# Queries, gates and output projection multiplied as three passes over split operands, with two weight areas lent to the split parts

## The chip, the cores and the metric

The kernel runs on one core of one Trainium2 chip. The time is the device time of one execution in microseconds (us), as the median of three runs. The profile is of one further execution, taken by the hardware profiler. Engines are called by their names in the profile: PE is the matrix engine (PEld are its weight loads), DVE the vector engine, ACT the scalar engine, POOL the general engine, SP the engine that issues the weight transfers.

## The reference, cut to what matters

One transformer block on 256 tokens of 1024 features, all in float32. Queries, two gates and the output projection are plain matrix products; a mixture of 32 experts follows, of which each token uses 4, and every expert's weights (12 MB) are read.

```python
p = h @ w_in[l]                                   # keys and values, then queries and gates
q_a, q_b, g_a, g_b = split_qg(p[..., KV_COLS:])   # 512, 512, 1024, 1024 columns
...
y_a = global_attn(q_a, ...);  y_b = window_attn(q_b, ...)
x = x + g1 * (sigmoid(g_a) * (y_a @ w_br_a) + sigmoid(g_b) * (y_b @ w_br_b)) @ w_o
h2 = modulate(rms_norm(x, norm2_g[l]), sh2, sc2)
x = x + g2 * moe(h2, ...)                         # for e in range(32): t @ w_e1[e] ... act @ w_e2[e]
return rms_norm(x, final_g)
```

## The kernel before

**The stream of weights.** All weights go through a ring of areas in on-chip memory, each 128 x 4096 floats (2 MB), filled in a fixed order (`pieces`) by the SP queue. `N_PAIR = 8` areas are there from the start, each split in two halves of 1 MB; a front piece (`m0`, `q`, `in`, `mod`, `br`, `wo`) takes one half, an expert piece (`w1`, `w2`) a whole area. `done()` gives a piece's place back and `pump()` issues the next transfer into it, in program order; SP then waits until the last reader of that place has finished. After the attention `grow(xx)` and `grow(ptt)` add two more areas, so the experts run on ten.

**The front, in program order.** (1) The modulation `m0_prod(j)`/`m0_turn(j)` makes the scaled input `x[:, j, :]`, two rows of the loop ahead, between the query products `q_prods(j)`: 8 rows j x 8 column groups, each a product of a 128x128 weight block with 128x256 of x. (2) `q_chunk` rotates the queries on DVE while PE makes `gate(0)` and `gate(1)`; then keys (`proj`) and values. (3) `gate(2)` to `gate(8)`; a gate is 8 products of 128x128 by 128x256 and a Tanh on ACT. (4) The attention loop over u = 0 to 7 and two query halves qt: `turn` transposes the probabilities, `scores(u + 1, qt)` makes the next ones (maximum on DVE, Exp on ACT), `y_steps` finishes the last head pair, `weigh(u - 1)`, half a gate, `norm_p` (a reciprocal on DVE that needs the Exp's sums), and the share of the second modulation matrix (`mod_v` on DVE, `mod_p` on POOL and `mod_a` on ACT). (5) `br_prod`/`merge` multiplies the heads by `w_br`, weighs with the gates and leaves M. (6) The output projection: 8 groups m of 8 products, with `stats(m)` one group behind. (7) Routing, `gather`, and the experts: `gemm1`, `act`, `gemm2`, `scatter`.

Every engine runs its instructions in program order (`manual_schedule`); waits are semaphores that the framework sets from the data. A float32 product shows as two MATMUL records in the trace, each with its own weight load.

## Time and profile before

| what | value |
|---|---|
| median of 3 runs | 1195.11 us (1194.88 to 1195.83) |
| the profiled execution, its own time | 1195.13 us |
| its span, first to last instruction | 1193.4 us |
| PE busy | 1142.9 us (96%) |
| DVE, ACT, POOL busy | 359.4, 139.5, 35.7 us |
| moved by DMA | 458.34 MB, mean 384 GB/s |

The busy time of PE counts overlapping records once and their ends are modelled, so a busy PE is not yet a PE that sets the end. Between the span and the execution's own time lie 1.7 us, which are kept as they are.

### The profile page before, as it was taken

Reading aid. Unit: us, or ns where it says so; the run is one execution under the profiler, and the core shown is the slowest. Engines: PE = TensorE matmul, PEld = TensorE weight load, DVE = VectorE, ACT = ScalarE, POOL = GpSimd, SP = SyncE. Lnnn points to the kernel's source line nnn. Section 1 sums busy time; section 2 is a strip of 40 time slices with the busy share of each in tenths; the row PEclk is TensorE's granted clock in tenths of the full one; section 3 lists DMA queues with packets and bytes.
Section 4 is the critical chain, followed back from the end, with each engine's and each line's share of the span. In section 5 each row is a group of like instructions: output and inputs, shape, how many; then the busy total and the mean of one; then the engine's idle time right before and its main releaser. Section 6 shows DMA issues by size and latency. Waiting matters only on the chain.

```text
span 1193.4 us, 13447 instructions
## 1 busy us (share of the span) xinstructions
PE 1142.9 (96%) x5722; PEld 539.0 (45%) x5722; DVE 359.4 (30%) x767; ACT 139.5 (12%) x313; POOL 35.7 (3%) x31
## 2 busy tenths in 40 slices
PE   7999999999999999999999999999898989899996
PEld 5888666884434333443434343434232424233334
DVE  3274666332122232222232222222221212121222
ACT  2122554012000000000000000000000000000012
POOL 0232000000000000000000000000000000000001
PEclk9999999999999999999999999999999999999999
DMA  9995634948999999999999999999999999999994
GB/s 378 383 387 211 225 128 153 390 177 351 427 429 426 428 426 428 429 427 428 426 429 426 429 426 428 427 428 428 428 427 427 428 428 426 429 427 429 425 428 181
DMA packets 37952, 458.34 MB, mean 384 GB/s; under 512 B 4600, under 2 KB 4992, under 8 KB 7424
## 3 DMA queue, kind: packets, MB, share of 16 engines
q1 hardware_dynamic: 36144, 454.05, 91.0%
q10 hardware_dynamic: 1744, 3.38, 0.7%
q8 instruction: 47, 0.77, 0.3%
q14 instruction: 17, 0.14, 0.0%
HBM read 456.36 MB, written 1.05 MB: 383 GB/s over the span
## 4 chain that ended last, share of the span: by engine, by line
PE 57%; DMA 36%; DVE 4%; ACT 2%; issue 1%; ACTq 0%; SPq 0%; DVEq 0%
DMA ring<-w 26%; PE u L845 20%; DMA xx<-w 10%; PE y L884 9%; PE mm L375 3%; PE xg L812 3%; PE u L695 3%; PE qa L276 2%; PE o L705 2%; PE sp L901 2%; PE br L579 2%; ACT xx L517 1%; PE yl L985 1%; PE kp L365 1%; PE vp L449 1%; DVE st L507 1%
## 5 line engine op out<-in xcount | busy, mean ns | idle before, releaser
L845 PE MATMUL u<-ring,t 128*64 128x512 f32 x1632 | 373.8, 598 | 16.1 <-DMA ring<-w 15.7
L845 PEld LDWEIGHTS u<-ring,t 128*64 128x64 f32 x1632 | 112.6, 137 | 233.3 <-issue 201.2
L884 PE MATMUL y<-ring,r_q 128*64 128x512 f32 x768 | 168.9, 592 | 0.0
L891 DVE TENSOR_TENSOR t<-y,r_kv 64x512 f32<-64x512 f32 x60 | 41.3, 689 | 325.3 <-PE y L884 324.9
L884 PEld LDWEIGHTS y<-ring,r_q 128*64 128x64 f32 x768 | 55.2, 137 | 109.6 <-issue 107.9
L858 DVE TENSOR_SCALAR r_q<-u 128x512 f32<-128x512 f32 x32 | 22.1, 692 | 248.6 <-PE u L845 248.6
L860 ACT ACTIVATE r_q<-r_q 128x512 f32<-128x512 f32 x32 | 20.1, 629 | 510.0 <-DVE r_q L858 510.0
L695 PE MATMUL u<-mtx,keep 128*64 128x512 f32 x256 | 62.2, 604 | 3.0 <-DVE r_q L861 3.0
L812 PEld LDWEIGHTS xg<-mtx,r_y 128*128 128x128 f32 x512 | 58.4, 192 | 12.2 <-issue 12.2
L812 PE MATMUL xg<-mtx,r_y 128*128 128x128 f32 x512 | 61.3, 278 | 0.0
L375 PE MATMUL mm<-xx,ring 128*128 128x256 f32 x256 | 59.9, 385 | 0.0
L901 PE MATMUL sp<-t,mtx 128*128 128x512 f32 x120 | 59.7, 620 | 0.0
L375 PEld LDWEIGHTS mm<-xx,ring 128*128 128x128 f32 x256 | 47.3, 190 | 12.6 <-issue 5.0
L845 PE MATMUL u<-xx,t 128*64 128x512 f32 x208 | 48.7, 610 | 3.7 <-DMA xx<-w 3.6
L845 PE MATMUL u<-ptt,t 128*64 128x512 f32 x208 | 48.8, 598 | 0.9 <-DMA ptt<-w 0.9
L814 DVE TENSOR_TENSOR t<-xg,modb 128x512 f32<-128x512 f32 x32 | 22.1, 692 | 86.3 <-PE xg L812 86.3
L901 PEld LDWEIGHTS sp<-t,mtx 128*128 128x128 f32 x120 | 20.5, 191 | 39.5 <-issue 39.5
L902 DVE TENSOR_TENSOR r_t<-r_t,sp 128x512 f32<-128x512 f32 x60 | 38.3, 680 | 0.0
L695 PEld LDWEIGHTS u<-mtx,keep 128*64 128x64 f32 x256 | 16.3, 135 | 44.6 <-issue 22.6
L874 ACT COPY r_q<-ta 128x512 f32<-128x512 f32 x32 | 18.8, 586 | 146.6 <-PE ta L871 146.6
L276 PE MATMUL qa<-xx,ring 128*128 128x256 f32 x128 | 30.7, 388 | 0.0
L845 PEld LDWEIGHTS u<-xx,t 128*64 128x64 f32 x208 | 14.7, 139 | 35.3 <-issue 28.1
(229 smaller groups left out, 897.4 us busy)
## 6 DMA issues: line engine op xcount, KB each, us to landing
ring<-w SPq DMA_DIRECT2D x149, 2048.0 KB, 32.4
xx<-w SPq DMA_DIRECT2D x19, 2048.0 KB, 31.0
ptt<-w SPq DMA_DIRECT2D x19, 2048.0 KB, 32.4
ring<-w_mod SPq DMA_DIRECT2D x16, 1024.0 KB, 11.2
ring<-w_in SPq DMA_DIRECT2D x10, 1024.0 KB, 9.1
ring<-w_m SPq DMA_DIRECT2D x8, 1024.0 KB, 12.6
ring<-w2l SPq DMA_DIRECT2D x3, 2048.0 KB, 34.3
ring<-w_q SPq DMA_DIRECT2D x8, 512.0 KB, 12.1
```

What stands on the lines that cost most here:

```text
L276: nc.tensor.matmul(qa[c // 4][:, c % 4, :], w[:, 128 * c:128 * c + 128], x[:, j, :], start=(j == 0 and c % 2 == 0), stop=(j == 7), skip_gr ...
L375: nc.tensor.matmul(gp[0][:, 0:256], w[:, k, :], x[:, k, :], start=(k == 0), stop=(k == 7))
L579: nc.tensor.matmul(ps[:, 0:256], w[:, k, 128 * (m % 2):128 * (m % 2) + 128], Y[:, 4 * br + k, :], start=(k == 0), stop=(k == 3))
L695: nc.tensor.matmul(u[c0:c0 + 64, ch % 2, :], ident[:, 4 * e + ch:4 * e + ch + 1].to_broadcast([128, 64]), be1, start=True, stop=False)
L705: nc.tensor.matmul(ps[:, 0:256], w[:, k, :], M[:, k, :], start=(k == 0), stop=(k == 7))
L812: nc.tensor.matmul(xp[:, b, :], z[:, tb, 128 * k:128 * k + 128], S[:, tb, :], start=(tb == 0), stop=(tb == 1))
L814: nc.vector.tensor_tensor(out=XT[p][:, 4 * h:4 * h + 4, :], in0=xp, in1=sh2[:, 4 * h:4 * h + 4].unsqueeze(2).to_broadcast([128, 4, 128]), ...
L845: nc.tensor.matmul(u[c0:c0 + 64, ch % 2, :], XT[p][:, k, 64 * j:64 * j + 64], w[:, 512 * ch:512 * ch + 512], start=False, stop=(k == 7))
L884: nc.tensor.matmul(y[64 * h:64 * h + 64, :], l, w[:, 512 * h:512 * h + 512], start=(k == 0), stop=(k == 7))
L891: nc.vector.tensor_tensor(out=YY[p][64 * j:64 * j + 64, 512 * h:512 * h + 512], in0=y[64 * h:64 * h + 64, :], in1=g2[64 * h:64 * h + 64, 5 ...
L901: nc.tensor.matmul(sp, t[:, tb, :], y[:, s], start=True, stop=True)
L902: nc.vector.tensor_tensor(out=ACC[0][:, tb, s], in0=ACC[0][:, tb, s], in1=sp, op=ALU.add)
```

## The change

Each operand x, the 32 weight pieces concerned, and M are split into an upper part, a copy by ACT into the type `float32r`, and a lower part, the remainder, which DVE subtracts. `mm3` makes each product as three matmuls in that type: upper by upper, upper by lower, lower by upper. The parts of weights lie in two buffers of 128 x 2048 in turn (`upper`, `prep`), made one group before they are used; a weight piece is given back to the ring as soon as its last part is made. Keys, values, `w_br` and the experts stay float32. The parts take 32 KB of a partition, which are two of the ring's areas: `N_PAIR` falls to 6 and the two come back as `more0` and `more1` after the output projection. In the attention loop `mod_v` now stands before `norm_p`.

```diff
-N_PAIR = 8
+N_PAIR = 6
...
+    room = ExitStack()
     fr = ExitStack()
+    fz = fr.enter_context(tc.tile_pool(name="fz", bufs=1))
...
+    cut = {}
+    X3 = [fz.tile([128, 2048], F32R, name=n, tag=f"part{i}").rearrange("p (k c) -> p k c", k=8)
+          for i, n in enumerate(("x_hi", "x_lo"))]
...
+    def lower(lo, v, hi):
+        nc.vector.tensor_tensor(out=lo, in0=v, in1=hi.bitcast(F32), op=ALU.subtract)
...
+    def upper(kind, idx, b, pool):
+        w = take(kind, idx)[:, 1024 * b:1024 * b + 1024]
+        hl = parts(None, 2, "part", 2 + n_cut[0] % 2, pool)
+        n_cut[0] += 1
+        nc.scalar.copy(out=hl[:, 0, :], in_=w)
+        cut[kind, idx, b] = hl
+
+    def prep(kind, idx, b):
+
+        w, hl = take(kind, idx)[:, 1024 * b:1024 * b + 1024], cut[kind, idx, b]
+        lower(hl[:, 1, :], w, hl[:, 0, :])
+        if b or kind == "q":
+            done(kind, idx)
...
+    def mm3(ps, lt, rt, start, stop, **kw):
+        nc.tensor.matmul(ps, lt[0], rt[0], start=start, stop=False, **kw)
+        nc.tensor.matmul(ps, lt[0], rt[1], start=False, stop=False, **kw)
+        nc.tensor.matmul(ps, lt[1], rt[0], start=False, stop=stop, **kw)
...
+        nc.scalar.copy(out=X3[0][:, j, :], in_=x[:, j, :])
+        lower(X3[1][:, j, :], x[:, j, :], X3[0][:, j, :])
...
     crow_half(0)
     crow_half(1)
+    upper("q", 0, 0, fz)
+    prep("q", 0, 0)
     for k in range(8):
...
     for j in range(8):
         if j < 6:
             m0_prod(j + 2)
+        if j < 7:
+            upper("q", j + 1, 0, fz)
         q_prods(j, range(4))
+        if j < 7:
+            prep("q", j + 1, 0)
         if j < 6:
             m0_turn(j + 2)
         q_prods(j, range(4, 8))
-        done("q", j)
...
+    gate_up(0)
+    gate_low(0)
     q_chunk(0)
+    gate_up(1)
     q_chunk(1)
+    gate_low(1)
     gate(0)
...
     gate(3)
+    gate_up(5)
+    gate_low(5)
     mod_a()
     gate(4)
...
     scores(0, 0)
     gate(7)
     scores(0, 1)
+    gate_low(8)
+    gate_up(9)
     mod_v()
     norm_p(0, 0)
     norm_p(0, 1)
+    gate_low(9)
     gate(8)
...
             nc.vector.tensor_tensor(out=M[:, m, :], in0=M[:, m, :], in1=dst, op=ALU.add)
+            nc.scalar.copy(out=M3[0][:, m, :], in_=M[:, m, :])
+            lower(M3[1][:, m, :], M[:, m, :], M3[0][:, m, :])
...
+            if u < 7 and qt:
+                gate_low(10 + u)
+            mod_v()
             if u < 7:
                 norm_p(u + 1, qt)
-            mod_v()
+            if not qt:
+                gate_up(10 + u)
...
     for m in range(2, 8):
+        if m in (2, 5):
+            upper("wo", 0, m // 4, mz)
         merge(1, m)
+        if m in (2, 5):
+            prep("wo", 0, m // 4)
...
         pend = (m, zt)
+        if m < 6:
+            upper("wo", m // 2 + 1, m % 2, mz)
+            prep("wo", m // 2 + 1, m % 2)
...
+    room.close()
+    lz = late.enter_context(tc.tile_pool(name="lz", bufs=1, reuse_waits="tile"))
+    for i in range(2):
+        grow(lz.tile([128, 4096], F32, name=f"more{i}"))
```

## Rows read from the trace of the kernel before

**Rows 1.** The page: 40 slices of the span for PE, DMA and bandwidth.
```profile
PE   7999999999999999999999999999898989899996
...
DMA  9995634948999999999999999999999999999994
GB/s 378 383 387 211 225 128 153 390 177 351 427 429 426 428 426 428 429 427 428 426 429 426 429 426 428 427 428 428 428 427 427 428 428 426 429 427 429 425 428 181
```

**Rows 2.** Windows by stage: stretch, length, busy of PE, PEld, DVE, ACT, POOL; clock, DMA.
```profile
19.10:55.50 36.40, 36.40 (x236) 28.78 (x233) 9.76 (x31) 4.91 (x12) 6.15 (x4) 1.00 0.96 387
...
97.50:124.00 26.50, 26.50 (x120) 21.49 (x120) 8.28 (x14) 9.60 (x21) 7.06 (x3) 1.00 0.77 278
124.00:196.30 72.30, 69.66 (x442) 47.18 (x441) 47.21 (x99) 38.06 (x99) 2.37 (x1) 1.00 0.45 161
...
232.70:264.70 32.00, 32.00 (x173) 28.70 (x172) 10.81 (x29) 4.48 (x13) 0.00 (x0) 1.00 0.51 196
...
730.00:1138.00 408.00, 387.53 (x1802) 141.97 (x1798) 95.32 (x178) 19.62 (x35) 0.00 (x0) 1.00 1.01 427
```

**Rows 3.** Windows around the first expert product, same columns.
```profile
265.00:275.00 10.00, 9.99 (x80) 7.64 (x81) 5.00 (x27) 6.54 (x14) 0.22 (x1) 1.00 0.90 340
275.00:277.60 2.60, 2.60 (x16) 0.89 (x14) 2.36 (x13) 0.00 (x0) 0.00 (x0) 1.00 0.02 9
277.60:279.60 2.00, 2.00 (x12) 0.61 (x10) 0.00 (x0) 0.00 (x0) 0.00 (x0) 1.00 0.71 131
```

**Rows 4.** The chain that ended last, in order of time: start, length, what.
```profile
97.49 17.27 PE mm L375 x80
...
222.35 10.36 PE br L579 x48
...
248.60 3.46 PE o L705 x16
...
270.50 3.57 PE xg L812 x32
274.08 7.02 PE u L845 x32
```

**Rows 5.** The same chain, later.
```profile
823.24 39.08 DMA ring<-w
```

**Rows 6.** Groups of instructions by shape, first 290 us: busy us, mean ns, idle before.
```profile
L375 PEld LDWEIGHTS mm<-xx,ring 128*128 128x128 f32 x256 | 47.3, 190 | 12.6 <-issue 5.0 <-ACT t L377 0.8 <-ACT xx L517 0.8
...
L333 DVE SCALAR_TENSOR_TENSOR ring<-ring,crow 128x1024 f32<-128x1024 f32 x22 | 26.3, 1211 | 0.0
...
L346 ACT ACTIVATE ring<-ring 128x1024 f32<-128x1024 f32 x10 | 10.6, 1063 | 0.0
...
L377 ACT ACTIVATE t<-mm 128x256 f32<-128x256 f32 x16 | 6.2, 390 | 17.9 <-PE mm L375 17.9
...
L238 ACT COPY msb<-mp 128x256 f32<-128x256 f32 x8 | 3.0, 373 | 28.6 <-PE mp L235 24.8 <-issue 3.7
...
L587 DVE TENSOR_TENSOR r_t<-r_t,t 128x256 f32<-128x256 f32 x8 | 3.4, 425 | 0.3
```

**Rows 7.** Timeline of the start: start, length, engine, line, instruction.
```profile
15.75 0.42 DVE L266 TENSOR_TENSOR xx<-xx,rinv 128x256 f32<-128x256 f32 x1
...
17.01 0.59 ACT L257 COPY crow<-cps 128x512 f32<-128x512 f32 x1 [1.25 <-PE cps L255]
...
19.11 1.99 PE L276 MATMUL qa<-xx,ring 128*128 128x256 f32 x8
```

**Rows 8.** Timeline of two half turns in the attention loop, u = 3 to 4.
```profile
165.70 0.37 ACT L558 COPY r<-y 128x256 f32<-128x256 f32 x1
...
166.10 0.42 DVE L559 TENSOR_TENSOR r_y<-y,r 128x256 f32<-128x256 f32 x1 [1.75 <-ACT r L558]
...
166.71 1.21 DVE L333 SCALAR_TENSOR_TENSOR ring<-ring,crow 128x1024 f32<-128x1024 f32 x1
...
169.97 0.69 ACT L517 ACTIVATE xx<-s,st 128x512 f32<-128x512 f32 x1 [2.10 <-DVE st L512]
...
171.54 0.16 DVE L526 TENSOR_TENSOR st<-st 128x2 f32<-128x2 f32 x1 [1.49 <-ACT st L520]
...
171.82 1.20 DVE L333 SCALAR_TENSOR_TENSOR ring<-ring,crow 128x1024 f32<-128x1024 f32 x1
```

More of the change, by code (lines that the diff above doesn't have):

```diff
@@ L273, in q_prods @@
     def q_prods(j, cs):
-        w = take("q", j)
+        w = cut["q", j, 0]
         for c in cs:
-            nc.tensor.matmul(qa[c // 4][:, c % 4, :], w[:, 128 * c:128 * c + 128], x[:, j, :],
-                             start=(j == 0 and c % 2 == 0), stop=(j == 7), skip_group_check=True)
+            mm3(qa[c // 4][:, c % 4, :], [w[:, i, 128 * c:128 * c + 128] for i in range(2)], [v[:, j, :] for v in X3],
+                start=(j == 0 and c % 2 == 0), stop=(j == 7), skip_group_check=True)
     hc_pend = []
@@ L372, in gate_half, with gate_up, gate_low @@
             gp[0] = ps1.tile([128, 512], F32, name="mm", tag=tag, bufs=bufs)
-        w = take("in", i)[:, 1024 * b:1024 * b + 1024].rearrange("p (k c) -> p k c", k=8)
+        w = parts_of("in", i, b)
         for k in range(4 * n, 4 * n + 4):
-            nc.tensor.matmul(gp[0][:, 0:256], w[:, k, :], x[:, k, :], start=(k == 0), stop=(k == 7))
+            mm3(gp[0][:, 0:256], [v[:, k, :] for v in w], [v[:, k, :] for v in X3], start=(k == 0), stop=(k == 7))
         if n:
             nc.scalar.activation(out=tanh[m // 4][:, m % 4, :], in_=gp[0][:, 0:256], func=AF.Tanh, scale=0.5)
-            if b:
-                done("in", i)
+    def gate_up(m):
+        if m < 16:
+            upper("in", 2 + m // 2, m % 2, fz)
+    def gate_low(m):
+        if m < 16:
+            prep("in", 2 + m // 2, m % 2)
     def gate(m):
@@ L469, in tile_dit_block @@
     values(2)
+    gate_up(2)
+    gate_low(2)
     mod_p()
@@ L472, in tile_dit_block @@
     values(3)
+    gate_up(3)
+    gate_low(3)
     mod_v()
@@ L476, in tile_dit_block @@
     gate(2)
+    gate_up(4)
+    gate_low(4)
     mod_v()
@@ L479, in tile_dit_block @@
     gate(3)
+    gate_up(5)
+    gate_low(5)
     mod_a()
     gate(4)
+    gate_up(6)
+    gate_low(6)
     mod_v()
     gate(5)
+    gate_up(7)
+    gate_low(7)
     mod_v()
@@ L486, in tile_dit_block @@
     gate(6)
+    gate_up(8)
     mod_p()
```

15 lines of the change are left out of this document (11 added, 4 removed).

## Prediction

> **What bounds the kernel now.** I read the 40 slices first. DMA runs at 425 to 429 GB/s from slice 11 to the last but one, and below that in every slice from the fourth to the tenth, down to 128 [rows 1]. The reader is to see two regimes: a front in which the stream stands still because its areas are full, and experts in which it never does. The chain says the same of the end: its late links are transfers of 39 us each [rows 5], while PE has 20 us of idle time between 730 and 1138 us and DMA none [rows 2]. So the experts end when the last bytes land, and the only time that can be won lies in the front. The hinge is the first expert product, which starts at 274.08 [rows 4]. All ten areas are full by 275, DMA falls to 9 GB/s, and after two steps of that product, at 277.6, the first area comes free and the stream starts for good [rows 3]. Everything ahead of 277.6 that gets shorter moves the end by as much, provided that the same ten areas are then full.
>
> In that front PE is busy without a gap in the queries, gates 2 to 8 and the output projection (36.4, 26.5 and 32.0 us) and almost so in the attention loop (69.66 of 72.3) [rows 2]. In the loop DVE and ACT are at 47 and 38 of 72 us and hand work to each other, so there PE's share alone decides little.
>
> **A product as three passes.** 80 records of the gates take 17.27 us [rows 4]; two records make a product, so it costs 0.432 us, a record 0.216. No row shows a matmul of type float32r. It streams the same 256 columns. A record's 0.216 us are two cycles a column at the granted 2.4 GHz level (clock 1.00 in every stage of [rows 2]); I bound a pass below by one cycle a column, 0.108, and above by a whole record, 0.216. What lies between is whether its weight load hides. Each record of 128x128 loads 128 columns too, with a mean of 190 ns [rows 6], yet the 32 records of the gather, which stream only 128 columns, follow each other every 3.57/32 = 0.112 us [rows 4]. So loads overlap and one costs at most 0.112 of PE's time. I take 0.112 per pass: 0.335 per product, 0.097 less than now. On 64 query, 128 gate and 64 output products that is 6.2, 12.4 and 6.2, together 24.8 us of PE; 0.78 per gate or output group. At the lower bound it is 27.6, at the upper one PE gains 55 us of work.
>
> The Trainium skill ("FP8 and Floating Point Precision", TensorE Precision Notes) says that true FP32 takes four passes and that a reduced form reads four bytes and truncates; by it a pass is 0.432/4 = 0.108 and the saving 27.6 us. No run here shows it yet.
>
> **What the parts cost elsewhere.** An upper part of 1024 columns is an ACT copy, 1.06 us by the pass of the same size that ACT makes now; a lower part is two-operand DVE work of 1024 columns, 1.21. For 256 columns of x or M it is 0.37 and 0.42 [rows 6]. 32 weight parts and 16 slices make 40 us on ACT and 45 on DVE. They are hidden while PE's product lasts longer than the chain that makes the next parts; I go through the front by stage.
>
> *Start, +2.6.* `upper` of the first query piece follows the copy of crow that ends on ACT at 17.60, so it ends at 18.66 and its lower part on DVE at 19.9. In DVE's order the normalisation of x stands behind it, and that now starts at 15.75 [rows 7]. Then come x0's multiply, three steps of modulation (about 1.2 together), its copy and remainder; the first query product, now at 19.11, starts at about 21.7. If the scheduler's other waits hide it, nothing; if the piece lands late, 4.
>
> *Query products, -5.3.* PE saves 6.2. Per row j ACT has 1.06 + 2 x 0.37 and DVE 1.21 + 0.42 + about 0.8, partly in turn: a chain of some 3.6 us. PE's first six rows hold the modulation's products too: (36.4 - 2 x 3.45) / 6 = 4.9 now, 4.1 after, which covers it. The last two hold none and take 8 x 0.335 = 2.7; there PE waits about 0.9 (none to 2).
>
> *Gates 0 and 1 to the keys, -0.9.* Two gates save 1.55; the lower part of gate 1 stands behind two rotations on DVE and comes some 0.65 late. Keys and values are not touched.
>
> *Gates 2 to 8, -2.65.* Seven gates save 5.45. A buffer is free when its gate has ended; then follow on ACT the Tanh (0.39) and the copy, on DVE the remainder, with handovers some 2.9 us, against a gate of 2.68: about 0.2 lost on each of five gates. Gate 8's remainder is queued on DVE behind the two row maxima of the first scores, each 1.2; I take 1.8 there. Sum 2.8 lost.
>
> *Attention loop, -2.8.* Take two half turns. In the half with qt = 0, DVE waits 1.49 for the Exp's sums and then runs `mod_v` (1.20) [rows 8]; with the new order `mod_v` fills that wait, so the half is 1.2 shorter. In the other half the product that ends `y_steps` stands ahead in DVE's order and waits 1.75 for ACT's copy at 165.70, which itself follows the Exp [rows 8]. The swap gains nothing there, and `gate_low` adds 1.21 behind it. A turn comes out even, and what PE saves on its gate turns into waiting. Only in the first three turns, before the second branch's longer chain, do I count 0.9 each (between nothing and 0.78 + 1.21), together 2.8. The copies of `gate_up` are behind the Exp on ACT, and behind them waits only the next transposed copy, which has the reciprocal's time.
>
> *Output projection, -3.4.* Eight groups save 6.2. In the merges DVE now has per group 3 x 0.42 and a wait of 0.37 for ACT, with handovers 1.73, as much as PE's 10.36/6 [rows 4], and twice 1.21 for the first weight parts. M's last parts are 2 us late for the first output group, and the remainders of the later groups, behind each group's own DVE work, cost some 0.8. In the steady part PE's 2.7 and the 0.6 of `stats` cover the chain.
>
> Sum: 2.6 - 5.3 - 0.9 - 2.65 - 2.8 - 3.4 = -12.4 us at 264.7 and at 277.6.
>
> **The two areas.** I counted the pieces against the places given back, in program order: with 12 halves every front piece is still issued at least three gates or a turn of the loop before its use, since a place now comes back after DVE's remainder, one group ahead of PE, and SP waits for DVE there instead. The first expert piece goes out in turn 5 and the next as `xx` comes free, 50 us before their use. No cost. At the first expert product eight areas and the two returned ones must be full. The return is at the end of the output projection, 12.9 us before the stream's start, and in these 12.9 us DMA has to move 4.2 MB into them and the 1.3 MB that ACT's queue loads in the same stretch (`g2`, `fg`, `be2` by their shapes): 5.5 MB at 427 GB/s are 12.9. It just fits, and as the queue is then not empty the stream saves today's restart at 131 GB/s [rows 3]. I count nothing; the loss is at most 9.8 us, if both areas land only after the first one is freed.
>
> So 1195.13 of the profiled execution, 0.02 from the median, becomes 1182.7, rounded 1183.
>
> **The rivals.** (a) *The weight load does not hide under a single pass*: a pass costs a record, 0.216. PE then has 256 x 0.216 = 55 us more, all parts are covered, and the time is about 1195 + 55 = 1250, since the delay at the start is the only other cost left and the waits vanish. For it: a weight load reads 190 ns, longer than a pass. Against it: the gather's 0.112 with equal loads. It decides from about 0.13 per pass, where the 12.4 us of waits and delays (24.8 less 12.4) equal the saving. The Trainium skill ("TensorE: Matmul & The Clock Gate", Part 3, The mechanism) states a rule of this kind: a load overlaps a running matmul only when the row group differs, and here all rows are used. By it a pass of 256 columns would be 107 + 107 ns; the gather's rows disagree with it.
>
> (b) *The loop really shortens.* If `gate_low` (1.21) fits into the 1.75 us of waiting in the qt = 1 half, that half stays as it is and each turn is 1.2 shorter: 4 x 1.2 in the later turns and the full 1.99 instead of 0.9 in the first three, 8 us more, 1175. For it: DVE's idle time is there; against it: the order on DVE, where the waiting product stands ahead.
>
> (c) *The parts come late in the loop.* If `mod_v` does not slip under the Exp, six turns grow by 1.21: 1190.
>
> (d) *The areas come late.* Each us that the returned areas land too late is a us of stream; with 9.8 the time is 1193 and the change does nothing. For it: the fit above is without slack; against it: an unfinished transfer at 277.6 keeps the queue running.
>
> **How the numbers follow.** The forecast has 0.62, with its own range 1178 to 1189 (0.108 per pass and no loss at gate 8 on one side, -2.8 - 1.8; 0.12 per pass on the other, 256 x 3 x 0.008 = 6.2). (a) 0.13, (b) 0.12, (c) 0.07, (d) 0.06. What a measurement here can tell from no change is about 0.2%, 2.4 us. Faster: the forecast, (b) and most of (c), 0.79; same: (d) and a rest of (c), 0.08; slower: (a), 0.13. The range that leaves out (a) and part of (d) is 1174 to 1193.
>
> **What would show it.** The float32r records should follow each other every 0.112 us in a gate; 0.108 or 0.216 tells the bounds. The first query product should start near 21.7, the loop's turns keep about 10.8 us apart with PE waiting in them, gate 8 wait for DVE, the output projection start 9 us earlier and its groups take 3.3. The first expert product should start at about 261.7, and DMA should not fall idle between the end of the output projection and the experts; the late links of the chain should still be transfers of 39 us. Wrong would be a chain in which DVE's remainders stand through the loop, or PE's passes longer than their columns.

## The result, and the profile after

The changed kernel takes 1205.53 us (median of 4 runs, 1202.81 to 1206.62), the kernel before 1195.25 on the same chip: ratio 1.0076, interval 1.0057 to 1.0095. It is slower by some 10 us where 1183 was forecast. The profiled execution has a span of 1204.5 us against 1193.4; the account below explains these 11.1 us.

The page, 40 slices of the span, of the changed kernel, answering to [rows 1]:
```profile
PE   6889898999999999999999999999898989899996
...
PEclk8989899999999999999999999999999999999998
DMA  9954655669999999999999999999999999999994
GB/s 378 372 213 158 246 212 189 234 243 414 428 428 427 427 428 429 426 428 428 425 427 429 428 427 428 429 426 426 429 428 427 428 428 428 427 427 427 429 427 165
```
The two regimes are still there: from slice 11 on the stream runs at 425 to 429 GB/s without a gap. But PE, full in slices 2 to 28 of before, has gaps in the front, and the granted clock falls in slices 1, 3 and 5.

The chain of the changed kernel, in order of time, answering to [rows 4, 5]: start, length, what.
```profile
64.86 3.31 DVE part L203
...
144.51 1.21 DVE part L203
...
155.17 1.13 DVE part L203
...
165.76 1.13 DVE part L203
...
282.51 7.02 PE u L935 x32
...
1050.11 39.12 DMA xx<-w
...
1143.12 35.64 DMA more<-w2l
```
The end is still set by transfers of 36 to 39 us. Ahead of them, eleven remainders of weights stand in this chain (L203 with `part`), 15.1 us together; four are shown, gate 1's and those of the first turns of the attention loop. The prediction named a chain with remainders through the loop as its sign of being wrong; they stand in it up to 167 us, and in no later turn. The first expert product starts at 282.51 in place of 274.08, 8.4 us later, and the end comes 922.0 us behind it in place of 919.3, another 2.7.

Windows of the changed kernel by stage, columns as in [rows 2]. The bounds are the starts of the first query product, gate 0, first key product, gate 2, first scores, first turn of the loop, merges, output projection; the last window ends with the projection:
```profile
22.73:57.82 35.09, 34.08 (x300) 30.17 (x297) 20.23 (x38) 15.02 (x26) 6.37 (x4) 0.94 0.95 378
57.82:74.10 16.28, 11.13 (x63) 10.27 (x61) 12.51 (x24) 4.86 (x8) 8.67 (x4) 0.79 1.01 425
...
106.20:120.90 14.70, 14.70 (x122) 14.57 (x120) 10.23 (x9) 10.28 (x16) 3.18 (x1) 1.00 0.70 265
120.90:135.20 14.30, 10.78 (x57) 8.75 (x57) 13.47 (x17) 5.78 (x12) 5.60 (x2) 0.80 0.66 253
135.20:221.40 86.20, 79.45 (x594) 57.76 (x593) 61.84 (x121) 47.98 (x117) 4.73 (x2) 0.99 0.55 201
221.40:242.10 20.70, 20.70 (x98) 18.17 (x97) 10.47 (x27) 6.10 (x11) 0.00 (x0) 1.00 0.78 284
242.10:273.70 31.60, 29.59 (x243) 28.43 (x241) 21.52 (x42) 11.44 (x24) 0.00 (x0) 1.00 0.68 244
```
In 106.20 to 120.90 (gates 2 to 6) PE works without a gap, and five gates take 14.70 us where 17.36 stood. PEld is busy for 14.57 of them. In 57.82 to 74.10 (gates 0 and 1, to the keys) PE stands for 5 of 16.28 us and the clock is 0.79; that stage took 9.5 before. In 120.90 to 135.20 (gates 7 and 8) DVE is busy for 13.47 of 14.30 us while PE stands for 3.5.

What PE waited for in the changed kernel, 15 to 290 us: total, times, longest.
```profile
PE mm L227 <- DVE part L203: 8.0, 3, 3.5
PE y L618 <- DVE r_y L628: 6.8, 6, 2.3
PE mtp L282 <- DVE mod L283: 2.9, 1, 2.9
```
The first row is the third pass of gates 0, 1 and 8 waiting for the weight's lower part, the third the start.

The timeline of the changed kernel around gates 0 and 1, and four passes of a gate: start, length, engine, line.
```profile
59.54 3.12 POOL L385 TENSOR_TENSOR ring<-ring,crow 128x1024 f32<-128x1024 f32 x1 [0.94 <-DMA ring<-w_mod]
...
60.68 0.41 DVE L404 TENSOR_TENSOR r_q<-qa,r_t 128x256 f32<-128x256 f32 x1
...
61.01 1.93 DVE L405 TENSOR_TENSOR sh<-sh,r_t 128x256 f32<-128x256 f32 x1
...
64.51 2.58 POOL L385 TENSOR_TENSOR ring<-ring,crow 128x1024 f32<-128x1024 f32 x1 [1.85 <-DMA ring<-w_mod]
64.78 3.38 DVE L203 TENSOR_TENSOR part<-ring,part 128x1024 fp32r<-128x1024 f32 x1
...
68.22 0.58 PE L227 MATMUL mm<-x_hi,part 128*128 128x256 f32 x1 [2.23 <-DVE part L203]
...
112.08 0.28 PE L227 MATMUL mm<-x_hi,part 128*128 128x256 f32 x1
112.20 0.28 PE L225 MATMUL mm<-x_hi,part 128*128 128x256 f32 x1
112.32 0.28 PE L226 MATMUL mm<-x_lo,part 128*128 128x256 f32 x1
112.44 0.28 PE L227 MATMUL mm<-x_hi,part 128*128 128x256 f32 x1
```
Gate 1's remainder starts on DVE at 64.78, 0.27 us after POOL's modulation product, and lasts 3.38 us; it ends 1.07 after POOL's. The rotation's L405, two operands in SBUF, lasts 1.93 beside POOL; L404, which has one operand in PSUM, 0.41. Passes follow each other every 0.12 us.

Groups of instructions by shape, 0 to 290 us, changed kernel, answering to [rows 6]: busy us, mean ns | idle before.
```profile
L203 DVE TENSOR_TENSOR part<-ring,part 128x1024 fp32r<-128x1024 f32 x32 | 41.5, 1296 | 24.7 <-ACT part L211 24.7
...
L211 ACT CAST part<-ring 128x1024 fp32r<-128x1024 f32 x32 | 33.4, 1044 | 2.5 <-DVE t L656 1.3 <-PE qa L227 1.1 <-ACT part L211 0.2
L379 DVE SCALAR_TENSOR_TENSOR ring<-ring,crow 128x1024 f32<-128x1024 f32 x22 | 31.1, 1418 | 0.0
```
The parts' own prices were right (1044 ns on ACT; DVE's median is 1225). DVE also stands idle for 24.7 us in all until ACT's copies end, so the two are made partly in turn. DVE is busy for 408.6 us in the span, 359.4 before: 49 us more for 9.3 us less of PE (1133.6).

The account, each stage by the starts on PE:

| stage | before | after | difference | forecast |
|---|---|---|---|---|
| to the first query product | 19.11 | 22.73 | +3.6 | +2.6 |
| query products | 36.40 | 35.09 | -1.3 | -5.3 |
| gates 0, 1, to the keys | 9.51 | 16.28 | +6.8 | -0.9 |
| keys and values | 32.30 | 32.12 | -0.2 | 0 |
| gates 2 to 6 | 17.36 | 14.70 | -2.7 | -2.65 (2 to 8) |
| first scores (gates 7, 8, loop) to merges | 96.94 | 100.47 | +3.5 | -2.8 (loop) |
| merges, projection, to the first expert | 62.4 | 61.0 | -1.4 | -3.4 |
| from there to the end | 919.3 | 922.0 | +2.7 | 0 |

### The profile page after: what moved, and what is told of

Read it like the earlier page. It is cut to its first block, busy times and chain, and to the rows that moved or that the text cites. A ratio compares the mean times of both kernels' runs of the same rounds, so it can differ in the third digit from the quotient of the medians.

```text
span 1204.5 us, 14068 instructions
## 1 busy us (share of the span) xinstructions
PE 1133.6 (94%) x5978; PEld 543.1 (45%) x5978; DVE 408.6 (34%) x815; ACT 175.8 (15%) x361; POOL 38.8 (3%) x31
## 3 DMA queue, kind: packets, MB, share of 16 engines
q10 hardware_dynamic: 1744, 3.38, 0.8%
## 4 chain that ended last, share of the span: by engine, by line
PE 50%; DMA 39%; DVE 6%; ACT 3%; issue 1%; ACTq 0%; SPq 0%; DVEq 0%
DMA ring<-w 20%; PE u L935 18%; PE y L974 9%; DMA xx<-w 6%; DMA more<-w 6%; DMA ptt<-w 3%; DMA more<-w2l 3%; PE u L780 3%; PE xg L902 2%; PE sp L991 2%; ACT xx L586 1%; DVE part L203 1%; PE kp L411 1%; PE vp L505 1%; DVE st L576 1%
## 5 line engine op out<-in xcount | busy, mean ns | idle before, releaser
L935 PE MATMUL u<-ring,t 128*64 128x512 f32 x1248 | 285.0, 596 | 14.3 <-DMA ring<-w 14.1
L935 PEld LDWEIGHTS u<-ring,t 128*64 128x64 f32 x1248 | 85.9, 137 | 179.9 <-issue 152.1
L974 PE MATMUL y<-ring,r_q 128*64 128x512 f32 x576 | 127.9, 592 | 0.0
L948 DVE TENSOR_SCALAR r_q<-u 128x512 f32<-128x512 f32 x32 | 22.1, 691 | 248.7 <-PE u L935 248.6
L950 ACT ACTIVATE r_q<-r_q 128x512 f32<-128x512 f32 x32 | 20.1, 630 | 510.2 <-DVE r_q L948 510.2
L935 PE MATMUL u<-more,t 128*64 128x512 f32 x384 | 87.5, 596 | 3.8 <-DMA more<-w 3.6
L974 PEld LDWEIGHTS y<-ring,r_q 128*64 128x64 f32 x576 | 41.3, 137 | 82.6 <-issue 79.1
L991 PE MATMUL sp<-t,mtx 128*128 128x512 f32 x120 | 59.5, 618 | 0.0
L904 DVE TENSOR_TENSOR t<-xg,modb 128x512 f32<-128x512 f32 x32 | 22.1, 691 | 88.0 <-PE xg L902 88.0
L935 PEld LDWEIGHTS u<-more,t 128*64 128x64 f32 x384 | 26.3, 137 | 54.8 <-issue 46.9
L203 DVE TENSOR_TENSOR part<-ring,part 128x1024 fp32r<-128x1024 f32 x32 | 41.5, 1296 | 24.7 <-ACT part L211 24.7
L227 PE MATMUL mm<-x_hi,part 128*128 128x256 f32 x128 | 39.2, 307 | 8.0 <-DVE part L203 8.0
L974 PE MATMUL y<-more,r_q 128*64 128x512 f32 x192 | 43.2, 592 | 0.0
L225 PE MATMUL mm<-x_hi,part 128*128 128x256 f32 x128 | 40.2, 314 | 0.0
L226 PE MATMUL mm<-x_lo,part 128*128 128x256 f32 x128 | 38.4, 300 | 0.0
## 6 DMA issues: line engine op xcount, KB each, us to landing
ring<-w_m SPq DMA_DIRECT2D x8, 1024.0 KB, 13.2
```

What stands on the lines that cost most here:

```text
L203: nc.vector.tensor_tensor(out=lo, in0=v, in1=hi.bitcast(F32), op=ALU.subtract)
L225: nc.tensor.matmul(ps, lt[0], rt[0], start=start, stop=False, **kw)
L226: nc.tensor.matmul(ps, lt[0], rt[1], start=False, stop=False, **kw)
L227: nc.tensor.matmul(ps, lt[1], rt[0], start=False, stop=stop, **kw)
L904: nc.vector.tensor_tensor(out=XT[p][:, 4 * h:4 * h + 4, :], in0=xp, in1=sh2[:, 4 * h:4 * h + 4].unsqueeze(2).to_broadcast([128, 4, 128]), ...
L935: nc.tensor.matmul(u[c0:c0 + 64, ch % 2, :], XT[p][:, k, 64 * j:64 * j + 64], w[:, 512 * ch:512 * ch + 512], start=False, stop=(k == 7))
```

## The experiments

The theory after the result: PE's share fell as planned, but the remainders on DVE come late, because DVE stands still while POOL works and because DVE has no 49 us to spare, and the areas come late besides. Rivals: the smaller ring is the whole loss; the passes themselves are no faster. In the table, "us" is the median of each kernel's runs and the ratio is to the kernel before on the same chip. The other columns, and the stages quoted below, are read from the one profiled execution of each, which can lie off the median (e11_pool_late by 3.4 us, e2_start by 3.1). e3, e4 and e10 leave work out, as their texts say. "Behind" is the time from the first expert product to the end, and "landed" what DMA had moved by 300 us (its mean rate in 0 to 300 us by 300).

| kernel | us | ratio to before, interval | first query | gate 0 to keys | scores to merges | first expert | behind | landed MB |
|---|---|---|---|---|---|---|---|---|
| before | 1195 to 1196 | | 19.1 | 9.5 | 96.9 | 274.0 | 919.4 | 83.7 |
| after | 1205.53 | 1.0076 (1.0057-1.0095) | 22.7 | 16.3 | 100.5 | 282.4 | 922.0 | 79.5 |
| e1_ring | 1204.73 | 1.0071 (1.0053-1.0088) | 19.6 | 9.5 | 99.5 | 277.4 | 925.0 | 80.4 |
| e2_start | 1207.59 | 1.0094 (1.0079-1.0108) | 22.1 | 15.4 | 104.7 | 286.4 | 922.6 | 78.0 |
| e3_no_low | 1183.93 | 0.9903 (0.9888-0.9919) | 18.8 | 8.4 | 96.1 | 260.8 | 921.4 | 89.1 |
| e4_pool | 1196.73 | 1.0005 (0.9996-1.0014) | 22.9 | 9.0 | 99.1 | 272.7 | 922.1 | 83.7 |
| e5_o_f32 | 1208.74 | 1.0095 (1.0080-1.0109) | 22.9 | 16.2 | 104.4 | 287.7 | 919.8 | 78.0 |
| e6_mod_dve | 1205.20 | 1.0065 (1.0052-1.0078) | 22.9 | 9.0 | 104.7 | 281.1 | 921.9 | 80.1 |
| e7_three | 1198.60 | 1.0018 (1.0008-1.0028) | 18.9 | 9.0 | 104.7 | 277.1 | 919.9 | 82.5 |
| e8_before_dve | 1204.82 | 1.0066 (1.0053-1.0079) | 19.5 | 9.5 | 105.0 | 282.5 | 919.3 | 80.1 |
| e9_early | 1191.31 | 0.9962 (0.9948-0.9976) | 21.1 | 10.4 | 94.3 | 271.4 | 920.1 | 84.9 |
| e11_pool_late | 1200.85 | 1.0035 (1.0022-1.0049) | 24.3 | 10.7 | 102.4 | 280.5 | 921.8 | 80.4 |
| e12_q0 | 1202.08 | 1.0042 (1.0029-1.0056) | 19.8 | 14.3 | 101.7 | 277.9 | 922.4 | 81.6 |
| e13_three_fix | 1200.96 | 1.0038 (1.0025-1.0051) | 21.0 | 8.7 | 103.1 | 278.0 | 922.0 | 81.6 |
| e14_best | 1189.78 | 0.9953 (0.9938-0.9968) | 19.9 | 8.7 | 93.2 | 268.1 | 919.9 | 86.4 |
| e15_low8 | 1207.72 | 1.0099 (1.0080-1.0119) | 23.0 | 12.7 | 103.5 | 281.3 | 922.5 | 80.1 |
| e16_fill | 1204.07 | 1.0077 (1.0054-1.0100) | 22.3 | 13.2 | 102.2 | 279.1 | 922.7 | 81.0 |
| e17_swap | 1192.31 | 0.9969 (0.9958-0.9980) | 19.2 | 9.5 | 93.8 | 270.9 | 919.6 | 85.2 |
| e18_no_pass | 1193.16 | 0.9976 (0.9967-0.9985) | 20.1 | 9.5 | 93.8 | 271.9 | 920.2 | 84.6 |

The last two columns are the master reading of the case: every kernel that has its eight areas before the experts ends 919.3 to 920.2 us behind its first expert product, every kernel with passes and the late return 921.4 to 922.7, and e1_ring, with the late return and no passes, 925.0. The ends follow the landed bytes: between e3_no_low and e5_o_f32 lie 11.1 MB, which at 427 GB/s are 26 us, and their spans differ by 25.3.

**e1_ring: the ring alone.**
```diff
-N_PAIR = 8
+N_PAIR = 6
...
+    lz = late.enter_context(tc.tile_pool(name="lz", bufs=1, reuse_waits="tile"))
+    for i in range(2):
+        grow(lz.tile([128, 4096], F32, name=f"more{i}"))
```


> The kernel before, with float32 products everywhere, and of the change the ring alone: six areas from the start, two more behind the output projection. If the smaller ring cost only what is seen behind the first expert product (the areas come late, 2.7 us of the 11.1), 1197 to 1198 us. If it also held up weights of the early stages and so most of the loss, 1201 us or more. If all of the loss is elsewhere (late remainders alone), 1195 us.

The ring alone costs 9.0 us, nearly as much as the whole change: 1201 or more came true, my 1197 to 1198 fell. That the ring is not the whole loss of the changed kernel shows in e3_no_low below, which has the same ring and is 21.6 us faster; no run has the parts and eight areas together. The first expert product is 3.4 us later and the end another 5.6. With parts that second share is only 2.7; what fits is that a weight split into parts gives its place back before its product, which `wo` in float32 does not, but no run separates this. Of the 3.4, 2.6 arise between first scores and merges. The timeline shows one stall there, in e1_ring:
```profile
142.25 2.35 POOL L339 TENSOR_TENSOR ring<-ring,crow 128x1024 f32<-128x1024 f32 x1 [8.50 <-DMA ring<-w_mod]
...
143.60 1.01 DVE L510 TENSOR_TENSOR st<-st,nrs 128x2 f32<-128x2 f32 x1
144.73 0.78 ACT L517 ACTIVATE xx<-s,st,rs 128x512 f32<-128x512 f32 x1 [3.74 <-DVE st L510]
...
147.13 0.66 PE L549 MATMUL y<-keep,st 128*64 128x128 f32 x8 [2.55 <-DVE r_y L559]
```
With six areas the modulation weight lands at 142 us, and POOL's product makes a DVE instruction of two columns last 1.01 us (0.16 elsewhere) just where the Exp waits for it. So a smaller ring also moves POOL's work to other places. The same is seen beside the passes: e3_no_low, without remainders, takes 96.1 us from scores to merges where e17_swap, with eight areas and no passes, takes 93.8, and there two such instructions of two columns last 1.82 and 1.92 us beside POOL.

**e2_start: the first query weights' parts behind the normalisation.**
```diff
-    upper("q", 0, 0, fz)
-    prep("q", 0, 0)
     for k in range(8):
...
             m0_turn(k // 2)
+    upper("q", 0, 0, fz)
+    prep("q", 0, 0)
```


> The changed kernel with both parts of the first query weights moved behind the normalisation of x and the first two modulation turns. If the start lost its 3.6 us because VectorE made that remainder first, and because TensorE then ran at the lower clock after its idle stretch, the first query product stands at about 20 us and the time falls by 3 us, to 1202.5. If later stages take the gain back (they wait for something else), 1205.

Missed. The first pass starts 0.6 us earlier, but the third then waits 1.0 us for its part: the edit swaps one late operand for another. The rest of its loss is between scores and merges (104.7), where its code is that of the changed kernel; e5_o_f32 below has the same loss, and its timeline shows from what.

**e3_no_low: no weight remainders.**
```diff
-        lower(hl[:, 1, :], w, hl[:, 0, :])
...
-        return [cut[kind, idx, b][:, i, :].rearrange("p (k c) -> p k c", k=8) for i in range(2)]
+        return [cut[kind, idx, b][:, 0, :].rearrange("p (k c) -> p k c", k=8) for i in range(2)]
```


> The changed kernel without the weights' lower parts: VectorE makes no remainder of a weight, and the third pass reads the upper part again. TensorE's passes, ring and ScalarE's casts stay. If late remainders on VectorE, and the lower clock after the waits for them, are the loss, gates 0 and 1 and gate 8 no longer wait, and the time falls by 8 to 12 us, to 1194 to 1197. If the passes themselves or the ring are the loss, it stays at 1203 to 1206.

It takes 21.6 us less than the changed kernel, about twice what was expected, with the same passes, copies and ring; in its trace PE never waits for a copy of a weight, so ACT is not what holds the passes up. So 32 instructions on DVE undo what the passes save. (A place in the ring also comes back a little earlier here, with the copy instead of the remainder; that share is not separated.) By stage the changed kernel has lost 4.0 us up to the first query product, 2.4 in the query products, 7.9 from gate 0 to the keys, 4.3 from scores to merges, 2.9 from there to the first expert product and 0.7 behind it. That 1183.93 is where the forecast put the change is a coincidence: the forecast had 24.8 saved and 12.4 lost again. Even so "behind" is 921.4: the late areas cost 2 us here too.

**e4_pool: short instructions on POOL.**
```diff
-        nc.gpsimd.tensor_tensor(out=w, in0=w, in1=crow, op=ALU.mult)
+        nc.gpsimd.tensor_tensor(out=w[:, 0:32], in0=w[:, 0:32], in1=crow[:, 0:32], op=ALU.mult)
```


> The changed kernel in which GpSimd multiplies 32 of the 1024 columns of its modulation weights instead of all (the rest of those sums is left out), so that its instructions are short. If VectorE's instructions with two operands in SBUF stand still while GpSimd's run, and that made the remainders of gates 1 and 8 late, these fall from 3.4 to 1.2 us, the rotation at 55 us from 4.3 to 1.2 us, and the time falls by 4 to 7 us, to 1199 to 1201. If it is only that VectorE has too much to do in that order, by 1 us at most.

It takes 8.8 us less than the changed kernel, more than expected, without one instruction less on PE or DVE. From gate 0 to the keys (window of e4_pool):
```profile
56.69:65.68 8.99, 8.20 (x62) 7.33 (x60) 6.66 (x21) 4.75 (x8) 1.54 (x2) 1.00 1.01 426
```
DVE does nearly the same work in 6.66 us busy (12.51 in the changed kernel's stage, which is longer), and the clock stays at 1.00.

**e5_o_f32: output projection in float32, areas given back after the loop.**
```diff
     fr.close()
+    lz = late.enter_context(tc.tile_pool(name="lz", bufs=1, reuse_waits="tile"))
+    for i in range(2):
+        grow(lz.tile([128, 4096], F32, name=f"more{i}"))
...
-            mm3(ps[:, 0:256], [v[:, k, :] for v in w], [v[:, k, :] for v in M3], start=(k == 0), stop=(k == 7))
+            nc.tensor.matmul(ps[:, 0:256], w[:, k, :], M[:, k, :], start=(k == 0), stop=(k == 7))
```


> The changed kernel with the output projection back in float32 (no parts of M, none of its weights), so that the two areas are given back when the attention loop ends, some 60 us earlier. If the end is set by the bytes that have landed when the transfers become continuous, the 4.2 MB of two areas are made up before that: 83 to 84 MB have landed at 300 us (79.6 in the changed kernel) and the time is 1194 to 1197 us. If only TensorE's late first expert product counts, the earlier return is worth nothing, and the projection's 0.58 us per group is lost against a shorter merge: 1203 to 1206 us.

The early return does give back its share: 919.8 behind the first expert product in place of 922.0. But that product is 5.2 us later, so only 78.0 MB have landed at 300 us, not 83 to 84: 1.3 us are lost in the float32 merges and projection, and 3.9 between scores and merges, ahead of everything that the edit changes. The timeline of e5_o_f32 shows where most of the 3.9 come from:
```profile
125.59 2.35 POOL L385 TENSOR_TENSOR ring<-ring,crow 128x1024 f32<-128x1024 f32 x1 [5.48 <-DMA ring<-w_mod]
125.79 2.16 DVE L579 TENSOR_TENSOR st<-st,nrs 128x2 f32<-128x2 f32 x1
...
128.67 2.35 POOL L385 TENSOR_TENSOR ring<-ring,crow 128x1024 f32<-128x1024 f32 x1 [0.74 <-DMA ring<-w_mod]
129.12 1.92 DVE L579 TENSOR_TENSOR st<-st,nrs 128x2 f32<-128x2 f32 x1
...
132.23 0.58 PE L227 MATMUL mm<-x_hi,part 128*128 128x256 f32 x1 [5.46 <-DVE part L203]
```
The first modulation weight lands 1.2 us earlier than in the changed kernel (125.6 for 126.8), and POOL's two products meet both of the two-column instructions that stand ahead of gate 8's remainder on DVE; there they met one (1.46). Gate 8 waits 5.5 us in place of 3.5. A third such meeting (1.44 at 153.41) costs a turn 0.9 us. After the last full turn PE waits 2.3 us for DVE in both kernels, but here the granted clock then falls to 0.53 for 3.5 us (1.00 in the changed kernel), which is another 1.7. e2_start has the same three (5.5, 1.0 and 1.6 us). So the loss of a stage depends on when a transfer lands, and a difference of 4 us there is not the edit's.

The total is worse than both theories said; only the "behind" column tells them apart.

**e6_mod_dve, e8_before_dve: all modulation sums on DVE**, in the changed kernel and in the one before.
```diff
     def mod_p():
-        t, w = mod_start()
-        nc.gpsimd.tensor_tensor(out=w, in0=w, in1=crow, op=ALU.mult)
-        mod_sum.append((t, w))
+        mod_v()
```


> The changed kernel with all 32 modulation sums on VectorE (22 before): GpSimd multiplies none. VectorE has 10 instructions of 1.21 us more. If a multiplication on GpSimd costs VectorE's two-operand instructions more than that (2.3 to 3.2 us of standing still), the early rotations and remainders take 1.1 and 1.2 us again, the first key product is at 70 us as with the short GpSimd instructions, and the time is 1197 to 1200 us. If VectorE's load is what counts, the turns of the loop grow beyond 10.8 us and the time is 1206 us or more.

> The kernel before with all 32 modulation sums on VectorE. If GpSimd's multiplications stand in VectorE's way there only off the path, nothing is gained: 1195 to 1198 us. If they cost it time too, 1190 to 1193 us, and the edit's gain in the changed kernel is not the passes' affair.

Neither number of e6 held (1205.20), but both mechanisms are there: gate 0 to the keys takes 9.0 us in place of 16.3, and from the scores to the merges 104.7 in place of 100.5. e8's 1204.82 lies outside both of its guesses: with no remainder at all, that stretch grows by 8.0 us, which is seven more sums of 1.21 less a little. So between scores and merges it is DVE's queue that sets the time, in the kernel before already. My reading of the loop as an exchange of waits, with room for 1.21 us a turn, was too kind.

**e7_three: e5, e6 and the first query product in float32 together.**

> Three edits of the changed kernel together: output projection in float32 with the areas given back after the attention loop, all modulation sums on VectorE, and the first of the eight query products (j = 0) in float32, so that no weight's remainder stands ahead of it. If the three losses are separate (areas 8 to 10 us, GpSimd's standing in the way 8, the start 3), 1184 to 1188 us, below the kernel before. If they are one loss seen three times (whichever is late last), no better than the best single edit: 1194 to 1197 us.

It takes 1198.6 us: the start and the areas are repaired, and the loop pays for POOL's work (104.7). Neither guess held.

**e11_pool_late and e12_q0: single repairs of the changed kernel.** The first holds POOL until gate 1's remainder is made, the second makes query product j = 0 in float32.
```diff
     gate_low(1)
+    pj = f1.tile([128, 1], F32, name="pj")
+    nc.gpsimd.tensor_copy(pj, cut["in", 2, 1][:, 1, 0:1].bitcast(F32))
     gate(0)
```
```diff
-    upper("q", 0, 0, fz)
-    prep("q", 0, 0)
...
+        if j < 1:
+            w = take("q", j)
+            for c in cs:
+                nc.tensor.matmul(qa[c // 4][:, c % 4, :], w[:, 128 * c:128 * c + 128], x[:, j, :],
+                                 start=(j == 0 and c % 2 == 0), stop=(j == 7), skip_group_check=True)
...
+            return
```


> The changed kernel with GpSimd's modulation products held until the remainder of gate 1 is made, nothing else. If GpSimd's products stood in VectorE's way there, the rotations and that remainder take 1.1 and 1.2 us, gate 0 to the keys takes 9 to 10 us (16.3 in the changed kernel), and the time is 1197 to 1200 us. If later collisions (gates 7 and 8) take it back, 1203 to 1206.

> The changed kernel with the first of the eight query products (j = 0) in float32, so that no remainder of a weight stands ahead of it. If the start's loss is that remainder, the first query product is at 18.9 us (22.7), its eight products cost 0.6 us more, and the time is 1202 to 1203 us. If gates 0 and 1 wait for VectorE whenever they come, the 3 us are waited out there: 1205.

They gain 4.7 and 3.4 us, both near the first of their two guesses. The timeline of e11_pool_late:
```profile
61.58 1.22 DVE L203 TENSOR_TENSOR part<-ring,part 128x1024 fp32r<-128x1024 f32 x1
...
63.00 7.41 POOL L385 TENSOR_TENSOR ring<-ring,crow 128x1024 f32<-128x1024 f32 x3
63.39 2.32 DVE L405 TENSOR_TENSOR sh<-sh,r_t 128x256 f32<-128x256 f32 x1
```
Gate 1's remainder lasts 1.22 once POOL is quiet, and the rotation that now runs beside POOL 2.32 in place of 0.41. The standing still goes wherever the two meet.

**e10_half: passes of 128 columns.** Only its trace is used, not its time.
```diff
-            mm3(gp[0][:, 0:256], [v[:, k, :] for v in w], [v[:, k, :] for v in X3], start=(k == 0), stop=(k == 7))
+            mm3(gp[0][:, 0:128], [v[:, k, :] for v in w], [v[:, k, 0:128] for v in X3], start=(k == 0), stop=(k == 7))
```


> The changed kernel with 128 columns of x instead of 256 in each pass of the gates (the second half of the positions is left out and its gate is a copy of the first). If a pass lasts as long as its weight load, its 0.12 us (start to start in gates 3 to 6) stays 0.12. If it lasts as long as its columns, it falls to 0.06.

The timeline of e10_half:
```profile
110.10 0.28 PE L227 MATMUL mm<-x_hi,part 128*128 128x128 f32 x1
110.22 0.27 PE L225 MATMUL mm<-x_hi,part 128*128 128x128 f32 x1
110.33 0.27 PE L226 MATMUL mm<-x_lo,part 128*128 128x128 f32 x1
```
Half the columns, and a pass still takes 0.11 us in place of 0.12, so the columns are not what sets it. What stays the same in both is the load of 128 weight columns, with PEld busy for 14.57 of 14.70 us in gates 2 to 6; that this load is the floor is argued, since no run changes its size.

**e13_three_fix and e15_low8: gate 8's remainder earlier.** e15 has this edit alone, e13 also the two repairs (POOL held until the keys are rotated) and the rotation tables scaled two query groups earlier.
```diff
     gate_up(8)
+    gate_low(8)
     mod_p()
...
     scores(0, 1)
-    gate_low(8)
```


> The changed kernel with all its passes kept and three places mended: first query product (j = 0) in float32; the scaling of the rotation tables two query groups earlier and GpSimd's modulation products held until the keys are rotated; gate 8's remainder made right behind its upper part. Single edits gave 3.4 us (start) and 4.7 us (GpSimd held), and gate 8 waited 3.5 us. If these three are the loss and add up, first query product 19.5 us, keys 63, scores 110, loop from 120, first expert product 267 to 269, and the time 1189 to 1192 us, below the kernel before. If one takes back what another gives, 1196 us or more.

> The changed kernel with gate 8's remainder made right behind its upper part instead of behind both scores and two modulation sums on VectorE. If gate 8's wait for it (3.5 us) is a loss of its own, the loop starts 11 us behind the first scores (14.3) and the time is 1201 to 1203 us. If the loop's first turn waits for the exponentials anyway, it stays at 1204 to 1206.

e13 came out as its second branch said (one takes back what another gives), e15 slower than both of its guesses. In e13 POOL's products now meet DVE's work for gates 2 and 6: gates 2 to 6 take 17.2 us in place of 14.7. In e15 the loop does start 9.4 us behind the first scores in place of 14.3, and then takes 94.1 us in place of 86.2. Gate 8's wait was no loss of its own; it is one place where DVE's backlog shows. (Of the 7.9 us that the loop lost, 1.7 are a lower clock at its end, as in e5_o_f32.) First scores to merges, window of e13_three_fix:
```profile
113.86:216.93 103.07, 91.42 (x649) 65.89 (x648) 73.30 (x135) 53.59 (x129) 10.01 (x4) 0.95 0.52 191
```
The same window of the changed kernel, and of e3_no_low without remainders:
```profile
120.93:221.40 100.47, 90.20 (x650) 66.51 (x649) 75.28 (x138) 53.76 (x129) 10.34 (x4) 0.97 0.56 208
```
```profile
106.56:202.70 96.14, 88.83 (x650) 64.65 (x649) 64.94 (x123) 53.69 (x129) 9.57 (x4) 0.98 0.57 209
```
DVE is busy for 73 to 75 us with remainders and 65 without, 59.5 before (in the old order of the loop); the stretch lasts 100 to 103, 96 and 97.

**e16_fill: products that nobody reads in the idle start.**
```diff
             m0_turn(k // 2)
+        if k == 0:
+            fil = ps1.tile([128, 512], F32, name="fil", tag="y")
+            for _ in range(7):
+                nc.tensor.matmul(fil[:, 0:256], ones, crow[:, 0:256], start=True, stop=True)
```


> The changed kernel with seven float32 products of 256 columns, whose result nobody reads, in TensorE's idle stretch of 17.2 to 20.1 us. If the lower granted clock at 20 to 30 us (0.53 and 0.79) comes from that stretch, it is 1.00 there, the first passes last 0.12 us instead of 0.21, gate 0 starts 2 us earlier, and the time is 1202 to 1204 us. If the clock falls for another reason, nothing moves: 1205 us or more.

Windows of the changed kernel, then of e16_fill:
```profile
20.00:25.00 5.00, 4.91 (x30) 3.63 (x31) 3.92 (x14) 2.03 (x4) 0.00 (x0) 0.53 1.01 412
25.00:30.00 5.00, 5.00 (x42) 4.28 (x41) 2.36 (x5) 1.05 (x3) 0.00 (x0) 0.79 1.03 422
```
```profile
20.00:25.00 5.00, 4.86 (x44) 3.93 (x44) 3.92 (x14) 1.97 (x4) 0.00 (x0) 1.00 1.00 409
25.00:30.00 5.00, 5.00 (x50) 4.28 (x50) 3.66 (x7) 1.68 (x4) 0.00 (x0) 1.00 1.03 422
```
With products in the idle stretch the clock stays at its upper level, and gate 0 starts at 55.85 in place of 57.82, the 2 us expected. In the total this is not resolved (1202 to 1212 us in six runs).

**e17_swap and e18_no_pass: the kernel before without any pass.** e17 takes only the loop's new order from the change; e18 adds the earlier rotation tables and POOL held until the keys are rotated.
```diff
+            mod_v()
             if u < 7:
                 norm_p(u + 1, qt)
-            mod_v()
```


> The kernel before with one line of the change alone: in the attention loop the modulation sum on VectorE stands ahead of the reciprocals of the next turn's sums. The version with float32 gates in the loop and this order had turns of 10.3 us, the kernel before 10.8. If the order is what shortens the turn, the loop falls from 87.6 to 84 to 85 us and the time by 3 us, to 1192 to 1193. If the areas or the earlier start did it, nothing moves: 1195 to 1197.

> The kernel before, all products in float32 and eight areas throughout, with the edits of the best version that are no passes: the loop's order, the rotation tables scaled earlier, GpSimd's products held until the keys are rotated. If the best version's 1189.8 us owes its gain to these alone, 1189 to 1191 us here. If its passes ahead of the loop are worth their cost (gates 2 to 7 and the query products, 2 to 3 us after the later start), 1192 to 1194.

First scores to merges in e17_swap, whose columns are those of [rows 2]:
```profile
114.75:208.52 93.77, 92.37 (x577) 64.43 (x577) 60.09 (x123) 46.49 (x121) 4.71 (x2) 1.00 0.51 186
```
That is 3.2 us less than before in this stretch and 3.4 in the total, as its first guess said: the change carried a gain that its remainders hid. e18's other two edits give nothing on their own (1193.16, its second guess).

**e9_early and e14_best: passes only ahead of the attention loop.** Queries j = 1 to 7 and gates 0 to 7 as passes, the rest float32, areas back behind gate 7, rotation tables earlier; POOL held until gate 1's remainder (e9) or until the keys are rotated (e14, whose edit is shown last).
```diff
     scores(0, 0)
     gate(7)
+    first.close()
+    lz = late.enter_context(tc.tile_pool(name="lz", bufs=1, reuse_waits="tile", side="right"))
+    for i in range(2):
+        grow(lz.tile([128, 4096], F32, name=f"more{i}"))
...
+    pj = f1.tile([128, 1], F32, name="pj")
+    nc.gpsimd.tensor_copy(pj, K[:, 1, 0:1])
```


> Three passes only in the query products j = 1 to 7 and in gates 0 to 7; the first query product, gates 8 to 15 and the output projection in float32, as in the kernel before; the two areas given back behind gate 7, before the attention loop; GpSimd's modulation products held until the remainder of gate 1 is made, and the scaling of the rotation tables two query groups earlier. With the stages seen so far (first query product 18.9 us, gate 0 at 53, keys at 62, scores at 109, loop from 118, 87.6 us long, first expert product 62.4 us behind it, end 919.5 us behind that) the time is 1187 to 1189 us, below the kernel before. If the loop waits for weights that six areas brought late, as in the ring run (90.2 us), 1190 to 1192. If what the passes save ahead of the loop is only waited out in it, 1195.

> The kernel with passes ahead of the attention loop alone and early areas (1191.3 us), with GpSimd's products held longer, until the keys are rotated. There the rotation of the queries still took 2.3 us twice while GpSimd ran and the keys waited 2.3 us. If that is GpSimd again, the keys start 9.0 us behind gate 0 (10.4) and the time is 1188 to 1190 us. If the later products on GpSimd now hold up gates 2 to 7 instead, 1191 us or more.

Both beat the kernel before; e14 by 0.47% (interval 0.32 to 0.62). e9's time is that of its second guess, but not for its reason: the loop takes 85.3 us, not 90.2, and the loss lies ahead of it (gate 0 at 55.9 instead of 53). In e14 the keys come 8.7 us behind gate 0, as expected. Its first expert product, by its chain:
```profile
268.15 7.02 PE u L943 x32
```
That is 5.9 us before [rows 4]. Of these, 3.1 are the loop's order (e17); the passes ahead of the scores bring 2.5 to 3.4 us by the medians (e14 against e17 and e18), though the intervals overlap or touch. More was there: gates 2 to 6 take 17.34 us in e14, as without passes (17.36), and 14.69 in e9, because POOL's products now meet the keys' rotation ahead of gate 2's remainder, and gate 6's remainder itself, in e14:
```profile
106.48 3.14 DVE L204 TENSOR_TENSOR part<-ring,part 128x1024 fp32r<-128x1024 f32 x1 [1.66 <-ACT part L212]
```

## Why the prediction was wrong

The bound was right: in every kernel of the table the end comes 919 to 925 us behind the first expert product. The step that failed is "What the parts cost elsewhere": *"They are hidden while PE's product lasts longer than the chain that makes the next parts."* I priced each part alone, at its undisturbed duration, and checked it against PE's time for the next product. I did not add it to what DVE already had to do, nor ask what else DVE would meet. The forecast had 12.4 us of waits and delays in all; e3_no_low puts the price of the weights' remainders alone at 21.6 us.

*A product as three passes.* 0.112 was near: 0.119 to 0.120 in the gates, so a product saves 0.072 and 256 of them 18.4 us, not 24.8. e10_half shows that the columns are not the reason; the weight load under each pass is left. And not all of that can be had: e3, without remainders, is 11.9 us shorter in the stages outside the attention and hardly shorter in it, where e8 shows PE is not what sets the time. Rival (a) is out. By the rule on row groups in the Trainium skill ("TensorE: Matmul & The Clock Gate", Part 3, The mechanism) a pass would last 0.21, an estimate with load and columns in turn; the measured 0.12 rules it out here.

*Start, +2.6:* +3.6, by the mechanism named. Not foreseen: PE's idle 2.9 us there are followed by a granted clock of 0.53 and 0.79. With the clock up, gate 0 starts 2.0 us earlier (e16), 0.4 of it ahead of the first query product and 1.6 in the query products.

*Query products, -5.3:* -1.3. Without remainders (e3) -3.7; with 0.072 a product 4.6 was to be had. The clock took 1.6 and a wait for the last query weights' remainder 1.0, where 0.9 stood in the forecast.

*Gates 0 and 1 to the keys, -0.9:* +6.8, the largest miss. I had the remainder 0.65 late behind two rotations; it was late because POOL's modulation products made it last 3.38 and the rotations 1.93 and more (e4, e11: 9.0 and 10.7 us). Such rows stood in the trace of before, off the path, and I did not ask what would meet them.

*Gates 2 to 8, -2.65:* the same figure stands for gates 2 to 6 alone, by luck: there the forecast had 3.9 us saved less about 0.2 a gate of waiting, the run has the smaller saving and hardly a wait. Gate 8 waits 3.5 us for its remainder, where 1.8 stood; gates 7 and 8 belong to the next term.

*Attention loop, -2.8:* from the first scores to the merges +3.5. The swap shortens it by 3.2 (e17, 93.8), e3 has 2.4 more than e17, and the remainders cost another 4.3 (100.5 against e3's 96.1). The later turns do keep 10.8 us, as forecast and as before: the swap's gain is spent on the remainders there. So rival (c), turns longer by 1.21, did not happen, and rival (b) neither; what the forecast lacked are the waits at gate 8 and in the first turns, and e8 shows that DVE's queue sets this stretch.

*Merges and output projection, -3.4:* -1.4. Mostly size: the smaller saving per product takes 1.6 of the 2.0 (64 x 0.025); the remainders cost 2.9 there (e3), where 2.8 stood.

*The two areas, 0:* +2.7. "It just fits" did not: rival (d) happened, with 2.7 of its 9.8. Nothing stood in the forecast for what six areas do to the time at which modulation weights land, and so to the meetings of POOL and DVE (e1, e5). e5, e9 and e14, with the areas back earlier, have 919.8 to 920.1 again.

What stays open: how the lower clock and the waits share the loss at gates 0, 1 and 8 (only the start was separated), and how much of the loss the six areas cause beside the passes, since no run has passes and eight areas.

## What to carry to other kernels

Moving work off a busy engine pays only if the receiving engine's queue has room for it in that stage, so add it to that queue's sum and look at every other engine that its instructions can meet: here such meetings also move with the time at which a transfer lands. In a kernel that ends in a saturated stream, price a buffer by the bytes that have not landed when the stream becomes continuous, and give it back before that point, not at it. When a change bundles several edits, try each alone: here one line gives 3.4 us by itself, and the change that holds it loses 10.

## What the runs showed of the hardware

DVE instructions with two operands in SBUF stand still while POOL's 1024-column product runs: 3.38 us in place of 1.22, even 1.01 in place of 0.16 for two columns; with one operand in PSUM 0.41 stays 0.41. The Trainium skill ("SBUF — State Buffer", SBUF: two separate sides) states this: VectorE and GpSimd share a port pair that whoever starts first holds for its whole instruction. The trace agrees, 2.58 + 1.22 less the 0.27 between the starts being 3.5, where 3.38 was measured.

A pass of 256 columns in `float32r` takes 0.12 us at the granted 2.4 GHz level, one of 128 columns 0.11, each with a load of 128 weight columns. After PE's idle stretch of 2.9 us the granted clock was 0.53 and a pass took 0.21, the 1.2 GHz level; with products in that stretch it stayed at 1.00.
